# Feed forward of a hybrid decoder layer: the first product by seven products of quarters in six of eight chunks, and both products in two parts of sixteen column blocks

## The chip, the cores and the metric

The kernel runs on one core of a Trainium2 chip. The metric is the device time of one execution in microseconds (us). The engines are named as in the profile: PE is TensorE, PEld its weight load, DVE is VectorE, ACT is ScalarE, POOL is GpSimd, SP is SyncE, which only issues DMAs.

## What is computed

One decoder layer on 2048 prompt tokens and 64 sample tokens of width 1024, in fp32. A mixer (a gated linear recurrence beside a short convolution) is followed by a LayerNorm, and that by a dense feed forward with 4096 hidden columns:

```python
    mix = jnp.einsum('btm,md->btd', jnp.concatenate([o.astype(x.dtype), yc], axis=-1), w_out)
    x = _layer_norm(ALPHA * x + mix, ln1_g, ln1_b)

    hid = jnp.square(jax.nn.relu(jnp.einsum('btd,df->btf', x, w_ff1)))
    x = _layer_norm(ALPHA * x + jnp.einsum('btf,fd->btd', hid, w_ff2), ln2_g, ln2_b)
```

The states of the recurrence and of the convolution are outputs too.

## The kernel before

**Tiling.** The prompt goes in four blocks of 512 tokens (`b` from 0 to 3); the sample's 64 tokens ride with block 1. Each block runs a mixer stage (projections `m1` to `m3` with the recurrence between them, then the output projection in two passes of two token tiles) and a feed forward stage. Precision: each fp32 operand is split into a high part (fp32r) and the rest, and each product is three matmuls (`mm3`, L230 to L232: high by high, high by low, low by high; `mm3_on`, L236 to L238, in the second product).

**Weights.** All weights come as units of 128 x 1024, in the order in which `add_unit` lists them. For each unit SP loads 512 KB into `st` (three buffers), ACT copies the high part to `wh` (L194, four buffers), and DVE subtracts to get `wl` (L201, four buffers). `weights(u)` keeps this three units ahead of PE.

**First product, before.** A unit is a column block `f` of 128 hidden columns, 32 in all, in eight chunks of four. The first eight blocks go in two passes of 256 tokens (`f0`, since the LayerNorm of the later token tiles is still under way), the other 24 in one pass of 512 tokens (in block 1: 256 and then 320, with the sample), eight `k` steps of three matmuls each. ACT takes relu and square of the result out of PSUM into `raw` (L1008, L1010), which holds a chunk as four slots (two halves of tokens by two halves of hidden columns) of 2 x 256 columns.

**Second product.** It is done by seven products of quarters instead of eight (`PRODUCTS`): tokens, hidden columns and output columns are halved, sums of quarters of the hidden values are multiplied with sums of quarters of the weights, and the results are added into the outputs with signs (`INTO`). The order is step by step, B21, B11, T4, T2, T1, B22, T3, each over all eight chunks, so that a step's two PSUM banks collect over the chunks. For each (step, chunk), `prepare` runs two products ahead: ACT copies a slot's high part `h` (L1040), POOL subtracts to get `l` (L1041), and DVE forms the next sum of hidden values in place (L1045, L1047, L1049; L990 forms the first when a chunk is done). At the end of a step DVE adds its banks into the residual (L1069, L1072).

**Sums of weights.** The sums T1 to T4 of quarters of the second weights are made once, in block 0, in DRAM: POOL issues eight DMAs per chunk, copies (L331) and accumulating DMAs (L329), 64 in all, two of them after each step of the mixer's main loop from step 4 on (`next(making, 0)`). They share POOL's queue with its instructions, which run in order: the inverse root in the recurrence's output norm (L683), that of the LayerNorm (L262), and `l`. Eight DMAs are in flight at most, since they take turns on eight semaphores and each waits for the one before it on its own.

**LayerNorm.** `norm_steps` gives ACT the scaling (L857), PE the transposes (L864) and DVE gain and bias of the transposed values (L867, L868), placed by hand between PE's units (`lnq`). The residual gets gain and bias on DVE in the second `f0` pass (`affine`, L913).

Of the kernel before, what the change touches and what calls it, by code (L numbers as in the profile page):

```python
# [13 lines left out]
ALU = mybir.AluOpType  # L14
# [34 lines left out]
X_PLACES = (("B21", 2), ("B21", 5), ("B11", 2), ("B11", 5), ("B22", 5))  # L49
# [4 lines left out]
def hybrid_step(ctx, tc, a, o):  # L54
# [111 lines left out]
    def unit_dma():  # L166
        src, _, cols, _, _ = units[at["dma"]]
        st = TOK() if at["dma"] < 6 else new((P, D), "st", 3)
        if at["dma"] < 2:
            for half in (slice(0, D // 2), slice(D // 2, D)):  # L170
                nc.sync.dma_start(st[:, half], src[:, half])
        else:
            nc.sync.dma_start(st[:, :cols], src)
        stages[at["dma"]] = st
        at["dma"] += 1
# [143 lines left out]
    sums = [{k: scratch.tile([P, D], F32, tag=f"{k}_{c}", bufs=1, name=f"{k}_{c}") for k in SUMS} for c in range(NCH)]  # L319

    def make_sums():
        def at(c, k):
            return a["w_ff2"][c * 4 + RAW[k]] if k in RAW else sums[c][k]

        for to, of, acc in (("T1", "B11", False), ("T3", "B22", False), ("T1", "B12", True), ("T3", "B12", True),
                            ("T2", "T3", False), ("T2", "B11", True), ("T4", "T2", False), ("T4", "B21", True)):
            for c in range(NCH):
                if acc:
                    g.dma_start(at(c, to), at(c, of), accum_op=ALU.add, max_dma_last_dim=4096)  # L329
                else:  # L330
                    g.dma_start(at(c, to), at(c, of), max_dma_last_dim=4096)  # L331
                yield
# [3 lines left out]
    for b in range(NB):  # L336
# [14 lines left out]
        pl["ff1"] = [(f, add_unit(a["w_ff1"][f])) for f in range(nf, NF)]  # L351
        pl["ff2"] = []
        pl["nc"] = NCH - 1 if b == NB - 1 else NCH
        nx = x_units(b + 1) if b + 1 < NB else []
        for step, _ in PRODUCTS:
            for c in range(pl["nc"]):
                pl["ff2"].append((step, c, add_unit(a["w_ff2"][c * 4 + RAW[step]] if step in RAW else sums[c][step])))
                if (step, c) in X_PLACES and nx:
                    src, cols, use = nx.pop(0)
                    add_unit(src, cols=cols, use=use)  # L360
# [11 lines left out]
    for b in range(NB):  # L372
# [468 lines left out]
        x1 = {}  # L841
# [3 lines left out]
        def norm_steps(tl):  # L845
# [13 lines left out]
            def flip(t, i):  # L859
# [5 lines left out]
                tmp = tmps[t, i] = TMP()  # L865
# [39 lines left out]
        affined = set()  # L905

        def affine(t, dh):
            if (t, dh) in affined:
                return
            affined.add((t, dh))  # L910
            z = x1[t][:tsz[t], dh * 512:dh * 512 + 512]
            for i, op in enumerate((ALU.mult, ALU.add)):
                v.tensor_tensor(z, z, lnb[:tsz[t], i, dh * 512:dh * 512 + 512], op)  # L913
# [65 lines left out]
        ncs = pl["nc"]  # L979
# [5 lines left out]
        rs = [TOK().rearrange("p (f t) -> p f t", t=NS) for _ in range(2)] if samp else None  # L985
# [6 lines left out]
        def ff1(f, w, sg):  # L992
# [3 lines left out]
            if c not in raw:  # L996

                raw[c] = F((P, 4, 2, 256), "raw", NCH)
            r = raw[c][:, 2 * odd:2 * odd + 2, q, :]
# [5 lines left out]
            a0, a1 = sg[0][0], sg[-1][0] + sg[-1][1]  # L1005
            for (c0, n), ps in zip(sg, banks):
                h0, h1 = c0 // 256, min(c0 + n, TB) // 256
                s.activation(r[:, h0:h1], ps[:, :256 * (h1 - h0)].rearrange("p (s t) -> p s t", t=256), AF.Relu)  # L1008
            h0, h1 = a0 // 256, min(a1, TB) // 256
            s.activation(r[:, h0:h1], r[:, h0:h1], AF.Square)  # L1010
            if a1 > TB:
                z = rs[f // 16][:, f % 16, :]
                s.activation(z, banks[-1][:, TB - sg[-1][0]:a1 - sg[-1][0]], AF.Relu)
                s.activation(z, z, AF.Square)
            written[c] += a1 - a0
            if written[c] == 4 * ncols and c < ncs:
                chunk_done(c)
            after()

# [4 lines left out]
        flush()  # L1024
        for t, dh in ((2, 0), (3, 0), (0, 0), (1, 0), (2, 1), (3, 1), (0, 1), (1, 1), (4, 0), (4, 1)):
            if t < nt:
                lnq += [([lambda t=t, dh=dh: affine(t, dh)], [])]
        for f, w in twice(pl["f0"], 1):
            ff1(f, w, [(256, ncols - 256)])

        queue = [(step, c) for step, c, _ in pl["ff2"]]
# [20 lines left out]

        for i, (f, u) in enumerate(pl["ff1"]):
            if i >= len(pl["ff1"]) - 2:
                prepare()
            ff1(f, weights(u), segs)
        drain()
        norm_weights(1)
        if b == 0:
            for _ in making:  # L1060
                pass
# [24 lines left out]
        spairs = []  # L1086
        squeue = [c * FC + 2 * SAMPLE[step][0] for step, c, _ in pl["ff2"] if samp and step in SAMPLE]

        def sample_rows():
            if squeue:  # L1090
                f = squeue.pop(0)
                hp = F((P, 2, P), "hp", 2, F32R)
                split(hp[:, :, 0:NS], hp[:, :, NS:P], rs[f // 16][:, f % 16:f % 16 + 2, :])
                spairs.append(hp)

        to = dict(PRODUCTS)
        banks = {}
        sample_rows()
        for step, c, u in pl["ff2"]:
            w = weights(u)  # L1100
            parts = [tuple(x[:, q * 512:q * 512 + 512] for x in w) for q in range(2)]
            prepare()
            if step in SAMPLE:
                sample_rows()
            if step == "T3" and pl["last"] and 2 <= c < 6:
                if c == 2:
                    last = [F((P, 4, 2, 256), "raw", NCH, F32R) for _ in range(2)]
                split(last[0][:, c - 2], last[1][:, c - 2], raw[NCH - 1][:, c - 2])
            k = to[step]
            first = k not in banks  # L1110
            if first:
                banks[k] = [PS() for _ in range(2)]
            h, l = hid.pop((step, c))
            for p in range(2):
                cs = slice(p * P, p * P + P)
                for q, (rh, rl) in enumerate(parts):
                    mm3_on(banks[k][p], h[:, q, cs], l[:, q, cs], rh, rl, first and q == 0, c == ncs - 1 and q == 1)
            if samp and step in SAMPLE:
                if c == 0:
                    ys = PS()  # L1120
                hp = spairs.pop(0)
                for q, (rh, rl) in enumerate(parts):
                    mm_pair(ys, hp[:, q, :], rh, rl, c == 0 and q == 0, c == ncs - 1 and q == 1)
            if c == ncs - 1:
                for t0, dh, sign in INTO[k][step]:
                    for p in range(2):
                        add_to(t0 + p, dh, banks[k][p], sign)
                if samp and step in SAMPLE:
                    sample_sums(ys, SAMPLE[step][1])
# [138 lines left out]
```

## Time and profile before

| | |
|---|---|
| time, median of 3 runs | 2449.0 us (2446.64 to 2449.62) |
| the profiled execution's own time | 2449.19 us |
| its span, first to last instruction | 2447.4 us |
| PE busy | 2400.3 us (98%), 12876 matmuls |
| DVE, ACT, POOL busy | 1542.2, 1114.9, 524.9 us |
| first product of block 0 in one pass | 304 to 434 us |
| second product of block 0 | 434 to 593 us |

The profile is one execution. Matmuls are pipelined, and a matmul's shown length is longer than the distance to the next, so what a stage costs is read from the distance between starts of like instructions, not from busy time. A wait is put down to what ended last. The timeline gives start, length, engine, line and tiles of an instruction, merged where several of one kind follow each other (x8); the waiting time before it and what ended it stand in brackets.

### The profile page before, as it was taken

To read this page: it belongs to the slowest core of one execution; us is meant where nothing else is said; L and a number is where in the kernel's file an instruction comes from. 1 tells how busy PE (TensorE), PEld (TensorE's weight loads), DVE (VectorE), ACT (ScalarE), POOL (GpSimd) and SP (SyncE) were. 2 spreads that over 40 slices of the span, in tenths; PEclk is the share of its full clock that TensorE was granted. 3 is DMA by queue.
4 is the path that set the end of the run, shared out by engine and by line. 5 is a ranking of instruction groups with operands and counts; after the bars stand their busy time and mean duration, and the time that the engine had idled before them with its cause. 6 is when DMAs were issued, how large, how long until landed. Compare 5 with 4: busy or idle time off the path is not lost. (4 is left out here: it accounts for less than half of the span.)

```text
span 2447.4 us, 32997 instructions
## 1 busy us (share of the span) xinstructions
PE 2400.3 (98%) x12876; PEld 2051.5 (84%) x12876; DVE 1542.2 (63%) x2153; ACT 1114.9 (46%) x1794; POOL 524.9 (21%) x376
## 2 busy tenths in 40 slices
PE   7999999999999999999999999999999999999998
PEld 5888988878889889998778888988878888988876
DVE  5756822696865684227968857623886865822597
ACT  4334534654324354445554244534654334543553
POOL 3210000654001110004750000001662001000554
PEclk9999999999999999999999999999999999999999
DMA  9985423655223633225543225423654324433453
GB/s 329 277 233 174 160 97 112 199 186 179 79 78 75 211 121 104 87 96 164 180 149 118 91 80 190 144 96 129 206 188 146 104 82 159 161 103 116 163 184 113
DMA packets 103548, 358.79 MB, mean 147 GB/s; under 512 B 11552, under 2 KB 16032, under 8 KB 103392
## 3 DMA queue, kind: packets, MB, share of 16 engines
q1 hardware_dynamic: 91216, 313.88, 38.6%
q0 software_dynamic: 12032, 42.54, 6.5%
q8 instruction: 101, 1.65, 0.3%
q14 instruction: 55, 0.45, 0.1%
q10 hardware_dynamic: 144, 0.26, 0.0%
HBM read 345.59 MB, written 44.60 MB: 159 GB/s over the span
## 5 line engine op out<-in xcount | busy, mean ns | idle before, releaser
L201 DVE TENSOR_TENSOR wl<-st,wh 128x1024 fp32r<-128x1024 f32 x514 | 679.5, 1325 | 548.3 <-ACT wh L194 547.5
L230 PE MATMUL ps<-X,wh 128*128 128x512 f32 (+2 forms) x2272 | 779.6, 343 | 14.2 <-ACT X L155 11.0
L232 PE MATMUL ps<-X,wl 128*128 128x512 f32 (+2 forms) x2272 | 769.4, 339 | 1.0 <-DVE wl L201 1.0
L231 PE MATMUL ps<-X,wh 128*128 128x512 f32 (+2 forms) x2272 | 769.4, 339 | 0.5 <-DVE X L156 0.5
L194 ACT ACTIVATE wh<-st 128x1024 fp32r<-128x1024 f32 x515 | 543.1, 1055 | 381.0 <-DMA st<-T 90.8
L1041 POOL TENSOR_TENSOR l<-raw,h 128x512 fp32r<-128x512 f32 x217 | 391.6, 1808 | 947.3 <-ACT h L1040 930.9
L230 PEld LDWEIGHTS ps<-X,wh 128*128 128x128 f32 x2272 | 431.6, 190 | 60.6 <-ACT X L155 13.0
L232 PEld LDWEIGHTS ps<-X,wl 128*128 128x128 f32 x2272 | 431.3, 190 | 43.7 <-DVE wl L201 1.9
L231 PEld LDWEIGHTS ps<-X,wh 128*128 128x128 f32 x2272 | 431.7, 190 | 42.1 <-DVE X L156 2.6
L238 PE MATMUL ps<-wh,l 128*128 128x512 f32 x868 | 342.1, 394 | 8.9 <-POOL l L1041 8.9
L236 PE MATMUL ps<-wh,h 128*128 128x512 f32 x868 | 339.1, 391 | 6.3 <-DVE tok L1072 5.0
L237 PE MATMUL ps<-wl,h 128*128 128x512 f32 x868 | 339.2, 391 | 1.6 <-DVE wl L201 1.6
L1008 ACT ACTIVATE raw<-ps 128x256 f32<-128x256 f32 (+1 forms) x184 | 85.7, 466 | 372.6 <-PE ps L232 370.9
L238 PEld LDWEIGHTS ps<-wh,l 128*128 128x128 f32 x868 | 163.3, 188 | 53.1 <-POOL l L1041 19.9
L236 PEld LDWEIGHTS ps<-wh,h 128*128 128x128 f32 x868 | 163.4, 188 | 40.7 <-issue 6.2
L237 PEld LDWEIGHTS ps<-wl,h 128*128 128x128 f32 x868 | 163.2, 188 | 37.4 <-DVE wl L201 3.3
L1040 ACT ACTIVATE h<-raw 128x512 fp32r<-128x512 f32 x217 | 133.5, 615 | 7.7 <-PE ps L237 5.7
L262 POOL TENSOR_TENSOR sm<-sm,nhalf 128x1 f32<-128x1 f32 (+1 forms) x34 | 36.5, 1075 | 383.4 <-DVE sm L261 383.4
L230 PE MATMUL ps<-wh,X 128*128 128x512 f32 x256 | 104.0, 406 | 0.0
L230 PE MATMUL ps<-wh,S 128*128 128x512 f32 x256 | 101.3, 396 | 0.0
L232 PE MATMUL ps<-wh,X 128*128 128x512 f32 x256 | 100.3, 392 | 0.0
L232 PE MATMUL ps<-wh,S 128*128 128x512 f32 x256 | 99.9, 390 | 0.0
(204 smaller groups left out, 2560.4 us busy)
## 6 DMA issues: line engine op xcount, KB each, us to landing
st<-in_w_ff SPq DMA_DIRECT2D x249, 512.0 KB, 3.3
st<-T SPq DMA_DIRECT2D x124, 512.0 KB, 3.3
st<-in_w_in SPq DMA_DIRECT2D x110, 512.0 KB, 3.3
st<-in_w_out SPq DMA_DIRECT2D x56, 512.0 KB, 4.3
T<-in_w_ff POOLq DMA_DIRECT2D x48, 512.0 KB, 19.7
T<-T POOLq DMA_DIRECT2D x16, 512.0 KB, 17.8
lnb<-in_lnb SPq DMA_DIRECT2D x16, 512.0 KB, 5.9
tok<-in_x SPq DMA_DIRECT2D x16, 512.0 KB, 6.9
```

The source lines that it names most:

```text
L194: s.activation(wh, st, AF.Copy)
L201: v.tensor_tensor(wl, st, wh.bitcast(F32), ALU.subtract)
L230: te.matmul(out, lh, rh, start=first, stop=False)
L231: te.matmul(out, lh, rl, start=False, stop=False)
L232: te.matmul(out, ll, rh, start=False, stop=last)
L236: te.matmul(out, lh, rh, start=first, stop=False, skip_group_check=True)
L237: te.matmul(out, lh, rl, start=False, stop=False, skip_group_check=True)
L238: te.matmul(out, ll, rh, start=False, stop=last, skip_group_check=True)
L262: g.tensor_tensor(st[:n, 15:16], st[:n, 14:15], nhalf[:n, 0:1], ALU.pow)
L1008: s.activation(r[:, h0:h1], ps[:, :256 * (h1 - h0)].rearrange("p (s t) -> p s t", t=256), AF.Relu)
L1040: s.activation(h, x, AF.Copy)
L1041: g.tensor_tensor(l, x, h.bitcast(F32), ALU.subtract)
```

## The change

- **First product.** The eight column blocks of chunks 0 and 1 (`NPLAIN = 2`) stay as they were. Chunks 2 to 7 go by the same seven products of quarters: the 1024 inputs, the four column blocks of a chunk and the 512 tokens are halved. Each product is a unit (eight groups of three matmuls, 256 tokens wide, or 320 with the sample in four of the seven), so 24 units of a block become 42. Results are combined on their way out of PSUM (`ff1_product`): copies with sign on ACT, additions on DVE, relu and square in one DVE instruction or two on ACT.
- **Sums of tokens.** In the second `f0` pass `sum_steps` forms the sums of quarters of the LayerNorm's output on DVE and splits them.
- **Sums of weights.** The same eight steps of sums are made for six chunks of the first weights, from rows of half the length, ahead of those of the second weights: 112 DMAs instead of 64, chunks 2 and 3 first. They begin two main loop steps later (`i >= 6`).
- **Two parts.** The feed forward runs as two parts of four chunks (`NPART = 4`): first product of chunks 2 and 3, second product of chunks 0 to 3, first of 4 to 7, second of 4 to 7. Each step's banks are added to the residual once a part. `raw` has four buffers instead of eight.
- **Residual's gain and bias** (`affine`) move from DVE to POOL, beside the first eight products.

The line numbers shift: L201 is L206 after the change, L683 is L706, L262 is L267, L1041 is L1197, L913 is L937, L331 and L329 are L347 and L345.

**POOL, block 0, end of the mixer.** What stands on its queue around the output norm's inverse roots, before (`T_6`, `T_7` are sums of chunks 6 and 7, `sm` small tiles):

```order
L329 DMA T_5_104<-in_w_ff 128x1024
L329 DMA T_6_108<-in_w_ff 128x1024
L329 DMA T_7_112<-in_w_ff 128x1024
L683 ISA
L683 TENSOR_TENSOR sm_1459<-sm_1459,nhalf 128x4
L683 TENSOR_TENSOR sm_1490<-sm_1490,nhalf 128x4
L683 TENSOR_TENSOR sm_1530<-sm_1530,nhalf 128x4
L683 TENSOR_TENSOR sm_1570<-sm_1570,nhalf 128x4
L262 TENSOR_TENSOR sm_1937<-sm_1937,nhalf 128x1
```

and after (`T_b` are sums of the second weights, `T_a` of the first):

```order
L345 DMA T_b_116<-in_w_ff 128x1024
L345 DMA T_b_120<-in_w_ff 128x1024
L706 ISA
L706 TENSOR_TENSOR sm_1505<-sm_1505,nhalf 128x4
L345 DMA T_b_124<-in_w_ff 128x1024
L345 DMA T_b_128<-in_w_ff 128x1024
L706 TENSOR_TENSOR sm_1536<-sm_1536,nhalf 128x4
L347 DMA T_b_129<-in_w_ff 128x1024
L347 DMA T_b_133<-in_w_ff 128x1024
L706 TENSOR_TENSOR sm_1578<-sm_1578,nhalf 128x4
L347 DMA T_b_137<-in_w_ff 128x1024
```

The first of the four now stands behind 78 sums, with two more ahead of each of the others; sixteen more follow the last, so that the LayerNorm's first L267 stands behind 100.

**POOL, block 0, from the first product to the second.** Before, the LayerNorm's last inverse roots are followed at once by the `l` of the second product:

```order
L262 TENSOR_TENSOR sm_2143<-sm_2143,nhalf 128x1
L262 TENSOR_TENSOR sm_2185<-sm_2185,nhalf 128x1
L1041 TENSOR_TENSOR l_3467<-raw_2149,h_3466 128x512
L1041 TENSOR_TENSOR l_3504<-raw_2311,h_3503 128x512
L1041 TENSOR_TENSOR l_3553<-raw_2735,h_3552 128x512
```

and after, from the second `l` of part one on:

```order
L1197 TENSOR_TENSOR l_3244<-raw_2378,h_3243 128x512
L345 DMA T_b_130<-in_w_ff 128x1024
L345 DMA T_b_134<-in_w_ff 128x1024
L345 DMA T_b_138<-in_w_ff 128x1024
L345 DMA T_b_142<-in_w_ff 128x1024
L347 DMA T_b_132<-T_b_130 128x1024
L347 DMA T_b_136<-T_b_134 128x1024
L347 DMA T_b_140<-T_b_138 128x1024
L347 DMA T_b_144<-T_b_142 128x1024
L345 DMA T_b_132<-in_w_ff 128x1024
L345 DMA T_b_136<-in_w_ff 128x1024
L345 DMA T_b_140<-in_w_ff 128x1024
```

One more DMA follows and then the third `l`: the last twelve sums (for chunks 4 to 7) stand between the second and the third.

The diff, cut to its core:

```diff
-X_PLACES = (("B21", 2), ("B21", 5), ("B11", 2), ("B11", 5), ("B22", 5))
+X_PLACES = (("B21", 4), ("B21", 6), ("B11", 4), ("B11", 6), ("B22", 5))
+NPLAIN = 2
+NPART = 4
...
     def make_sums():
...
+        for at, cs in ((quarter1, range(NPLAIN, NPART)), (quarter1, range(NPART, NCH)),
+                       (quarter2, range(NPART)), (quarter2, range(NPART, NCH))):
+            for to, of, acc in (("T1", "B11", False), ("T3", "B22", False), ("T1", "B12", True), ("T3", "B12", True),
+                                ("T2", "T3", False), ("T2", "B11", True), ("T4", "T2", False), ("T4", "B21", True)):
+                for c in cs:
+                    if acc:
+                        g.dma_start(at(c, to), at(c, of), accum_op=ALU.add, max_dma_last_dim=4096)
+                    else:
+                        g.dma_start(at(c, to), at(c, of), max_dma_last_dim=4096)
+                    yield
...
-            if b == 0 and i >= 4:
+            if b == 0 and i >= 6:
                 next(making, 0)
                 next(making, 0)
...
             for i, op in enumerate((ALU.mult, ALU.add)):
-                v.tensor_tensor(z, z, lnb[:tsz[t], i, dh * 512:dh * 512 + 512], op)
+                g.tensor_tensor(z, z, lnb[:tsz[t], i, dh * 512:dh * 512 + 512], op)
...
+        def ff1_product(step, c, w):
...
+            for kk in range(4):
+                for q in range(2):
+                    cs = slice(q * 512 + kk * P, q * 512 + kk * P + P)
+                    mm3_on(banks_[q][:, :n], wh[:, cs], wl[:, cs], xh_[:, kk, :n], xl_[:, kk, :n],
+                           first and kk == 0 and (q == 0 or len(banks_) == 2), kk == 3)
...
+        for part, (ff1_units, ff2_units) in enumerate(pl["parts"]):
+            queue += [(step, c) for step, c, _ in ff2_units]
+            for i, (step, c, u) in enumerate(ff1_units):
+                if i >= len(ff1_units) - 2:
+                    prepare()
+                ff1_product(step, c, weights(u))
+            drain()
+            if part == 0:
+                norm_weights(1)
+                if b == 0:
+                    for _ in making:
+                        pass
...
+            for step, c, u in ff2_units:
```

More of the change, by code (lines that the diff above doesn't have):

```diff
@@ L978, in hybrid_step, with sample_values, values @@
         raw, hid, written = {}, {}, [0] * NCH
-        ncs = pl["nc"]
         def F(shape, tag, bufs, dt=F32):
             return new(shape, tag, bufs, dt, phase["of"])
-        rs = [TOK().rearrange("p (f t) -> p f t", t=NS) for _ in range(2)] if samp else None
+        rs = {}
+        def sample_values(c, f):
+            part = c // NPART
+            if part not in rs:
+                rs[part] = TOK().rearrange("p (f t) -> p f t", t=NS)
+            return rs[part][:, f % (NPART * FC):f % (NPART * FC) + 2, :]
+        def values(c):
+            if c not in raw:
+                raw[c] = F((P, 4, 2, 256), "raw", NPART)
+            return raw[c]
         def chunk_done(c):
@@ new lines, in sum_steps, with parts, wide @@
+        def sum_steps():
+            (h0, h1), (l0, l1) = ([x[:, :, 0:256] for x in y] for y in x1g)
+            sa = F((P, 2, 4, 256), "raw", NPART)
+            s1, s2 = sa[:, 0], sa[:, 1]
+            r1, r2 = xr[0][:, 0], xr[0][:, 1]
+            def parts(key, src, wide, half, tiles):
+                xq[key] = tiles
+                split(*(x[:, :, 0:256] for x in tiles), src)
+                if wide and samp:
+                    for x, y in zip(tiles, x1g):
+                        s.activation(x[:, :, 256:], y[half][:, :, TB:TB + NS].bitcast(F32), AF.Copy)
+            def wide():
+                return [F((P, 4, 256 + NS), "sw", 4, F32R) for _ in range(2)]
+            v.tensor_tensor(s1, h1, h0, ALU.subtract)
+            yield
+            v.tensor_tensor(s1, s1, l1, ALU.add)
+            v.tensor_tensor(s1, s1, l0, ALU.subtract)
+            yield
+            parts("T1", s1, True, 0, wide())
+            v.scalar_tensor_tensor(s2, s1, -1.0, r1, ALU.mult, ALU.subtract)
+            yield
+            parts("T2", s2, False, 0, [TOK(F32R).rearrange("p (k t) -> p k t", k=4) for _ in range(2)])
+            v.scalar_tensor_tensor(r2, r2, -1.0, s2, ALU.mult, ALU.subtract)
+            yield
+            parts("B22", r2, True, 1, wide())
+            v.tensor_tensor(r1, r1, h0, ALU.subtract)
+            yield
+            v.tensor_tensor(r1, r1, l0, ALU.subtract)
+            parts("T3", r1, False, 0, [F((P, 4, 256), "sn", 2, F32R) for _ in range(2)])
+            xr.clear()
+            yield
@@ L1024, in hybrid_step @@
         flush()
+        making_sums = sum_steps()
+        for _ in range(6):
+            lnq += [([lambda: next(making_sums, 0)], [])]
+        for f, w in twice(pl["f0"], 1):
+            ff1(f, w, [(256, ncols - 256)])
+        drain()
         for t, dh in ((2, 0), (3, 0), (0, 0), (1, 0), (2, 1), (3, 1), (0, 1), (1, 1), (4, 0), (4, 1)):
@@ L1027, in hybrid_step @@
                 lnq += [([lambda t=t, dh=dh: affine(t, dh)], [])]
-        for f, w in twice(pl["f0"], 1):
-            ff1(f, w, [(256, ncols - 256)])
-        queue = [(step, c) for step, c, _ in pl["ff2"]]
+        queue = []
         def prepare():
@@ L1099, in hybrid_step @@
[L1099 to L1127, printed above, removed]
-                if samp and step in SAMPLE:
-                    sample_sums(ys, SAMPLE[step][1])
```

219 lines of the change are left out of this document (158 added, 61 removed).

## The prediction

> **What bounds the kernel now.** I read the page, then the profile by windows, then the timeline of the engines that the change loads.
>
> ```profile
> span 2447.4 us, 32997 instructions
> PE 2400.3 (98%) x12876; PEld 2051.5 (84%) x12876; DVE 1542.2 (63%) x2153; ACT 1114.9 (46%) x1794; POOL 524.9 (21%) x376
> DMA  9985423655223633225543225423654324433453
> ```
>
> TensorE is busy 98% of the span, so time falls only if TensorE issues less, and any new wait of TensorE adds to it. But the DMA engines are full in the first two to three of forty slices, the first 150 us or so. This is where the weight sums are built. How far apart matmuls are is read from ScalarE, which takes a finished unit out of PSUM (timeline of ScalarE: start, length, instruction):
>
> ```profile
> 300.58 0.38 ACT L1008 ACTIVATE raw<-ps 128x256 f32<-128x256 f32 x1 [1.10 <-PE ps L232]
> 303.46 0.38 ACT L1008 ACTIVATE raw<-ps 128x256 f32<-128x256 f32 x1 [1.10 <-PE ps L232]
> 308.92 0.60 ACT L1008 ACTIVATE raw<-ps 128x512 f32<-128x512 f32 x1 [3.68 <-PE ps L232]
> 314.36 0.60 ACT L1008 ACTIVATE raw<-ps 128x512 f32<-128x512 f32 x1 [3.23 <-PE ps L232]
> ...
> 940.45 0.39 ACT L1008 ACTIVATE raw<-ps 128x256 f32<-128x256 f32 x1 [1.33 <-PE ps L232]
> 943.97 0.39 ACT L1008 ACTIVATE raw<-ps 128x256 f32<-128x256 f32 x1 [1.34 <-PE ps L232]
> 949.93 0.83 ACT L1008 ACTIVATE raw<-ps 128x256 f32<-128x256 f32 x2 [3.77 <-PE ps L232]
> 956.33 0.83 ACT L1008 ACTIVATE raw<-ps 128x256 f32<-128x256 f32 x2 [3.56 <-PE ps L232]
> ```
>
> Each step is 24 matmuls, or twice 24 in the last pair: 256 wide 2.88 us, 512 wide 5.44, 320 wide 3.52, 256 and 320 together 6.40. So 256 columns cost 0.120 us, and twice that is 6% over the 0.227 us of 512.
>
> **Removed: TensorE work.** In blocks 0, 2 and 3, 24 units of 5.44 us (130.6) become 6 x 7 products of 2.88 us (121.0), 9.6 us less in each. In block 1 (with the sample) 24 x 6.40 = 153.6 becomes 24 x 3.52 + 18 x 2.88 = 136.3, 17.3 us less. In all 3 x 9.6 + 17.3 = **46.1 us**. The second product keeps its matmuls.
>
> The Trainium skill ("TensorE: Matmul & The Clock Gate", section "Back-to-back issue gap") has a rule against this: weight load and matmul together set the spacing, about 81 ns at 128 columns and 131 at 512. An estimate on the straight line between gives 98 ns at 256, by which the change would lengthen each first product; the rows above (0.120 against 0.227) say otherwise, so this way gets no chance.
>
> **Added: 48 more sums on GpSimd's queue in block 0.** GpSimd's timeline and the DMA tables:
>
> ```profile
> 1.34 4.30 POOL L331 DMA_DIRECT2D T<-in_w_ff  x8 [0.32 <-issue]
> 7.85 0.52 POOL L331 DMA_DIRECT2D T<-in_w_ff  x1 [2.22 <-DMA T<-in_w_ff]
> ...
> 22.87 0.52 POOL L331 DMA_DIRECT2D T<-in_w_ff  x1 [0.91 <-DMA T<-in_w_ff]
> ...
> 43.54 0.81 POOL L329 DMA_DIRECT2D T<-in_w_ff  x1 [2.83 <-DMA T<-in_w_ff]
> ...
> 67.72 0.81 POOL L329 DMA_DIRECT2D T<-in_w_ff  x1 [2.01 <-DMA T<-in_w_ff]
> ...
> 145.59 0.81 POOL L329 DMA_DIRECT2D T<-in_w_ff  x1 [1.79 <-DMA T<-T]
> 174.36 1.88 POOL L683 TENSOR_TENSOR sm<-sm,nhalf 128x4 f32<-128x4 f32 x1 [27.95 <-DVE sm L682]
> ...
> 234.36 0.55 POOL L262 TENSOR_TENSOR sm<-sm,nhalf 128x1 f32<-128x1 f32 x1 [43.81 <-DVE sm L261]
> ```
>
> ```profile
> q0 software_dynamic: 12032, 42.54, 6.5%
> ...
> T<-in_w_ff POOLq DMA_DIRECT2D x48, 512.0 KB, 19.7
> ...
> out_y<-tok POOLq DMA_DIRECT2D x12, 512.0 KB, 3.0
> ...
> out_y<-tok SPq DMA_DIRECT2D x7, 256.0 KB, 2.0
> ```
>
> Eight are in flight, and each later issue waits for the landing of one before it. Issues that wait on copies come (22.87 - 7.85) / 7 = 2.15 us apart, those on accumulations (67.72 - 43.54) / 7 = 3.45. The last of 64 lands near 145.59 + 19.7, say 168 us. Their work: queue 0 took 6.5% of 2447.4 = 159 us of all sixteen engines for 42.54 MB; the 64 sums are 33.55 MB of it, 125 us, so **1.96 us each**.
>
> GpSimd now meets its first L683 (L706 in the new code) behind 78 sums and its first L262 (L267) behind 100; before, both stood behind 64 that had landed. The hundredth waits until 96 have landed: 32 x 1.96 = 63 us of DMA work more than the 64. The 36 sums that touch quarters of the first weights go in rows half as long. That costs nothing if bytes count and 36 x 1.96 = 70 us if rows do; The output's halves from SP, 256 KB in such rows, land in 2.0 us against 3.0 for 512 KB in as many whole rows, so bytes count for most, and I take 5. The weights' own loads need, by the DMA share (columns: length, busy time of PE, its weight load, DVE, ACT, POOL, each with its count, clock, DMA share, GB/s):
>
> ```profile
> 175.00:200.00 25.00, 25.00 (x143) 21.54 (x142) 12.65 (x23) 15.11 (x52) 5.18 (x4) 1.00 0.26 88
> 200.00:215.00 15.00, 15.00 (x68) 12.39 (x67) 7.82 (x10) 5.28 (x6) 0.00 (x0) 1.00 0.57 208
> 215.00:235.00 20.00, 20.00 (x90) 16.57 (x89) 11.09 (x15) 5.89 (x6) 0.55 (x1) 1.00 0.68 236
> ...
> 435.00:457.00 22.00, 22.00 (x99) 18.19 (x98) 16.00 (x12) 14.95 (x20) 14.64 (x8) 1.00 0.67 209
> ```
>
> 6.5 + 8.6 + 13.6 us, and 1.8 for 168 to 175: 30.5. So L262 runs at 168 + 63 + 5 + 30 = 266 instead of 234: 32 us late. What hangs on both:
>
> ```profile
> 188.96 0.81 PE L692 MATMUL ps<-ident,S 128*128 128x128 f32 x5
> ...
> 235.65 1.23 ACT L857 ACTIVATE tok<-tok,sm 128x1024 f32<-128x1024 f32 x1
> ...
> L864 PE MATMUL ps<-ident,tok x32: 270/272/273, 239.9 to 274.4; 128*128 128x128 f32 x32
> ```
>
> L262 releases ScalarE's L857, done at 236.9, and behind L857 wait ScalarE's next weight splits; TensorE's transposes L864, which stand in its order in the middle of the output projection, start at 239.9. The slack is 3 us, so TensorE loses **29 us**. Half of it falls earlier: L683 waits for 74 landed sums (10 x 1.96 + 4 for short rows, and 8 for loads: 168 + 32 = 200 against 174), and ScalarE's scaling behind it, its own weight splits and TensorE's L692 with it; L692 starts at 188.96, some 10 us after it could (L683 ends at 176.2, and an estimated 2 to 3 us of ScalarE and VectorE lie between). What is lost there is part of the 29. Ends: 15, if the loads yield to the sums by half, and 29 + 65 with rows counting. SP's loads of the new sums pass no queue that holds them: chunks 2 and 3 are summed first.
>
> **Moved: twelve sums ahead of the second product.** They stand on GpSimd's queue between the second and the third `l` of block 0. Four accumulations, four copies that wait for them, four accumulations that wait for the copies. From 2.15 and 3.45 scaled to a mean of 1.96: 1.5 and 2.4 us of transfer. The first lands after about 4.5 (3.0 alone, a slower transfer, the issue), the fourth at 11.7, the copies from 13.2 to 17.7, the last issue ends at 18.5 and the third `l` (1.29 below) at 20; loads at share 0.67 add up to 4. Two `l` are ready, so TensorE needs it two products (12 matmuls of 0.227 us each, 2.72) and two matmuls later, at 5.9. It loses 14 to 18, I take **16** (6 if transfers overlap wholly, 20 at the first stage's pace).
>
> **Second product in two parts.** VectorE, by windows and by line in 479 to 545:
>
> ```profile
> 479.00:501.00 22.00, 21.71 (x96) 17.98 (x97) 21.73 (x18) 13.10 (x18) 14.14 (x9) 1.00 0.55 177
> 501.00:523.00 22.00, 21.38 (x91) 16.38 (x90) 22.00 (x19) 11.34 (x15) 10.05 (x7) 1.00 0.56 188
> 523.00:545.00 22.00, 21.06 (x90) 16.14 (x89) 22.00 (x18) 12.71 (x17) 12.14 (x9) 1.00 0.57 186
> ```
>
> ```profile
> L201 DVE TENSOR_TENSOR wl<-st,wh 128x1024 fp32r<-128x1024 f32 x23 | 41.8, 1818 | 0.0
> L1045 DVE SCALAR_TENSOR_TENSOR raw<-raw 128x512 f32<-128x512 f32 x8 | 12.0, 1504 | 1.2 <-POOL l L1041 1.2
> L1072 DVE SCALAR_TENSOR_TENSOR tok<-tok,ps 128x512 f32<-128x512 f32 x4 | 2.5, 675 | 0.0
> ```
>
> VectorE is full through T4, T2 and T1 (21.73, 22.00, 22.00 of 22), and TensorE idles 0.3, 0.6 and 0.9 us. Each part closes its banks with sixteen additions of 0.68 us, so a block gets sixteen more, eight of them (5.4 us) in that full stretch. But each part enters it after a slack one (16.00 of 22 in B21) and three units ahead. I take 2 us a block, **8** in all; ends 0 and 22.
>
> **First product's new vector work.** LayerNorm's scaling (L913) goes from VectorE to GpSimd beside the first eight products, in all sixteen instructions a block.
>
> ```profile
> L194 ACT ACTIVATE wh<-st 128x1024 fp32r<-128x1024 f32 x515 | 543.1, 1055 | 381.0 <-DMA st<-T 90.8
> ...
> L913 DVE TENSOR_TENSOR tok<-tok,lnb 128x512 f32<-128x512 f32 x64 | 43.7, 689 | 1.1
> ```
>
> ```profile
> 425.03 1.29 POOL L1041 TENSOR_TENSOR l<-raw,h 128x512 fp32r<-128x512 f32 x1 [160.74 <-ACT h L1040]
> ...
> L201 DVE TENSOR_TENSOR wl<-st,wh 128x1024 fp32r<-128x1024 f32 x22 | 27.2, 1236 | 90.7 <-ACT wh L194 90.7
> ```
>
> A chunk's seven products are 20.2 us of TensorE. VectorE then has seven splits, two squares that read SBUF alone, four additions out of PSUM and one difference: with GpSimd idle 7 x 1.24 + 7 x 0.68 = 13.4; at the durations beside a working GpSimd 7 x 1.82 + 2 x 1.50 + 5 x 0.68 = 19.1. Still below 20.2, so hidden but for edges: 1 us a block, **4**; ends 0 and 35 (the second rival). ScalarE has 7 x 1.06 for splits, four copies of 0.60 and two passes of a whole slot pair (1.06 each): 11.9. Loads come every 2.88 us, no denser than the second product's 2.72. The token sums take eleven VectorE instructions of 1.24 us, 13.6, under the second pass of 256 columns, where sixteen L913 of 0.69, 11.0, leave.
>
> **Sum:** -46.1 + 29 + 16 + 8 + 4 = +10.9. The profiled execution took 2449.19, the median is 2449.0, so **2460 us**. A measurement of this kernel can tell some 0.2%, 5 us, from no change.
>
> **Rivals.** *The sums are done in time (faster).* If GpSimd reaches L683 and L262 as early as now, only 16 + 8 + 4 stand against 46.1: 2431 us. Place: GpSimd's queue in block 0. It decides at the pace: 96 landed by 234 instead of 266 needs 32 us less of 188, 1.6 us a sum. For it: the mean of 1.96 includes other transfers of that queue. Against: the observed paces of 2.15 and 3.45 leave no room. 0.20.
>
> *VectorE becomes the bound (much slower).* If splits and GpSimd's instructions exclude each other, chunk 2 has 14 x 1.29 = 18.1 us of GpSimd and 11 of VectorE's SBUF work in 20.2 us: 8.9 late a block, 35 in all, 2491 us. For it: L201 grows from 1.24 to 1.82. Against: the second product holds its pace with both. 0.09. The Trainium skill ("SBUF — State Buffer", section "Who interferes with whom") states such an exclusive lock for a VectorE instruction with two SBUF inputs; the growth of L201 agrees in kind.
>
> *Short rows cost whole packets:* +65, 2525 us, 0.05. *Losses at their low ends* (15, 6, few us) meet the gain: near 2430 to 2449, I put it at no change, 0.08. That the products are not shorter is excluded by the rows above.
>
> **How the numbers follow.** Forecast 0.58, of which 0.05 ends within 5 us of 2449. Faster 0.20; same 0.08 + 0.05 = 0.13; slower 0.53 + 0.09 + 0.05 = 0.67. The range 2428 to 2490 holds the forecast's own ends, the no-change case, most of the faster one and half of the VectorE one; about 0.15 is left out.
>
> **What would show it.** Right: in block 0 the first L706 near 200 and L267 near 266, TensorE idle before L692 and L864; a gap of some 16 us after the second product of the second matmul stage; products 2.88 us apart; DMA full to about 260. Wrong: L267 near 235, or no gap at the third `l`, or products over 2.9 us apart with VectorE at 22 of 22.

## The result, and the profile after

The changed kernel takes 2554.1 us, median of 4 runs (2552.29 to 2559.95), beside 2447.8 for the kernel before, measured along with it: a ratio of 1.0441, 95% interval 1.0418 to 1.0464. The forecast was 2460, 2428 to 2490: the sign is right, the size is not. To the 106 us that it lost come the 46 us that TensorE's shorter products should have given, so about 152 us have to be found. (In ratios, which are used below because the kernel before differs by some 5 us between chips: 0.0441 x 2448 = 108.)

The page of the changed kernel, and from TensorE's waits (us in total, times, longest):

```profile
span 2558.2 us, 36164 instructions
PE 2389.6 (93%) x14028; PEld 2086.0 (82%) x14028; DVE 1816.3 (71%) x2479; ACT 1186.5 (46%) x1812; POOL 681.7 (27%) x492
PE   7995896998999997999989999999999999999997
PEclk9997998999999998999999999999999999999999
DMA  9999748555422452544454224465555324355553
q0 software_dynamic: 22016, 67.71, 10.6%
```

```profile
PE ps L243 <- POOL l L1197: 41.6, 26, 20.1
PE ps L715 <- DVE S L711: 26.8, 2, 24.2
PE ps L235 <- ACT X L160: 24.7, 8, 11.4
PE ps L241 <- ACT raw L1124: 13.4, 18, 1.3
PE ps L236 <- DVE X L161: 10.5, 5, 2.8
```

TensorE falls from 98% to 93%. The lowest slices after the first (5, 6 and 7 tenths) are the fourth and the seventh, in block 0, and the sixteenth, where block 1's feed forward begins, and in the same three the granted clock is below 9 tenths. About 10 us of the waits for X L160 come at the very start, where the kernel before has them too. The waits for L1124, here ScalarE's copy of T1's bank, are new and were not in the forecast.

The products themselves came as forecast. ScalarE takes them out 2.88 us apart, here T2 and T1 of one chunk (block 2; start, length, instruction):

```profile
1804.57 0.60 ACT L1124 ACTIVATE raw<-ps 128x512 f32<-128x512 f32 x1 [1.34 <-PE ps L243]
...
1807.44 0.60 ACT L1124 ACTIVATE raw<-ps 128x512 f32<-128x512 f32 x1 [1.25 <-PE ps L243]
```

A chunk of seven products takes longer than seven times 2.88, 20.16 us: B22's first matmuls of three chunks start at 1808.09, 1829.19 and 1850.29, 21.10 us apart, since each waits for that copy (e2).

**Block 0's mixer.** GpSimd's timeline: the first L706 (forecast near 200), the last sums of the mixer and L267 (forecast near 266). Behind it TensorE's wait, and two windows of the time after it (length, busy time of PE, its weight load, DVE, ACT, POOL, each with its count, clock, DMA share, GB/s).

```profile
209.67 1.37 POOL L706 TENSOR_TENSOR sm<-sm,nhalf 128x4 f32<-128x4 f32 x1
...
260.43 0.54 POOL L347 DMA_DIRECT2D T_b<-T_b  x1 [18.50 <-DMA T_b<-in_w_ff]
...
272.81 0.52 POOL L347 DMA_DIRECT2D T_b<-T_b  x1 [4.26 <-DMA T_b<-in_w_ff]
279.01 0.57 POOL L267 TENSOR_TENSOR sm<-sm,nhalf 128x1 f32<-128x1 f32 x1 [5.69 <-DVE sm L266]
```

```profile
212.99 1.12 PE L715 MATMUL ps<-ident,S 128*128 128x128 f32 x4 [24.23 <-DVE S L711]
```

```profile
230.00:255.00 25.00, 21.42 (x88) 17.09 (x87) 8.30 (x10) 4.51 (x5) 4.03 (x5) 0.93 1.04 310
255.00:280.00 25.00, 20.25 (x86) 15.45 (x84) 10.70 (x16) 5.58 (x5) 2.67 (x5) 1.00 1.04 335
```

The first L706 follows the 78th sum at once, 35 us later than the 174.36 of before. TensorE's L715 hangs on it through ScalarE and VectorE and starts 24 us late (188.96 before); with a second wait of 2.6 us the output projection starts 29 us late (238.75 against 210.00). So the forecast's 29 us are lost here already, where it had put half of them.

L267 runs 45 us later than the 234.36 of before, not 32, but not because of the sums ahead of it on GpSimd's queue: the last of them is issued at 272.81, and GpSimd then waits 5.69 us for VectorE's L266. The other 16 us are lost in the output projection. The DMA engines are full there (share 1.04, and 0.68 before), and between 238 and 280 us ScalarE waits 25.5 us for the projection's weights, which share these engines with the sums.

Queue 0 shows the size of the sums: 10.6% of 2558.2 is 271 us of all sixteen engines, against 159 before; 112 us for 48 sums are 2.34 us each, if all of it is put down to them, where the forecast had 1.96. That is 48 x 0.38 = 18 us more than at the forecast's price. All 48 stand ahead of the first L706, where the forecast had 4 us for short rows; it came 10 us later than 200.

**The seam.** GpSimd between the second and the third `l` of block 0, and TensorE behind it:

```profile
393.82 1.29 POOL L1197 TENSOR_TENSOR l<-raw,h 128x512 fp32r<-128x512 f32 x1 [0.17 <-ACT h L1196]
395.06 3.40 POOL L345 DMA_DIRECT2D T_b<-in_w_ff  x4
402.81 0.55 POOL L347 DMA_DIRECT2D T_b<-T_b  x1 [4.36 <-DMA T_b<-in_w_ff]
...
422.27 3.99 POOL L1197 TENSOR_TENSOR l<-raw,h 128x512 fp32r<-128x512 f32 x3
```

```profile
423.87 0.79 PE L243 MATMUL ps<-wh,l 128*128 128x512 f32 x1 [20.12 <-POOL l L1197]
424.46 0.63 PE L241 MATMUL ps<-wh,h 128*128 128x512 f32 x1
424.89 0.63 PE L242 MATMUL ps<-wl,h 128*128 128x512 f32 x1
...
428.26 0.39 PE L241 MATMUL ps<-wh,h 128*128 128x512 f32 x1
428.49 0.39 PE L242 MATMUL ps<-wl,h 128*128 128x512 f32 x1
```

The wait is 20.1 us, the upper end that the forecast gave. Behind it the matmuls start 0.43 us apart, and 0.23 only from 428.26 on: here the stall cost TensorE its own length and some 2 us at half clock.

**The two passes of 256 columns, block 1.** A window of the changed kernel from the end of the first pass into the second (columns as above), then VectorE's and GpSimd's groups in it (busy us, mean ns), and TensorE at the start of the second pass:

```profile
983.00:1013.00 30.00, 16.87 (x111) 16.12 (x110) 29.76 (x24) 10.77 (x21) 29.37 (x17) 0.72 0.22 72
```

```profile
L206 DVE TENSOR_TENSOR wl<-st,wh 128x1024 fp32r<-128x1024 f32 x4 | 8.1, 2022 | 0.0
L161 DVE TENSOR_TENSOR X<-raw,X 128x512 fp32r<-128x512 f32 x4 | 5.9, 1484 | 0.0
...
L896 DVE TENSOR_TENSOR raw<-ps,small 128x512 f32<-128x512 f32 x3 | 2.0, 677 | 0.0
```

```profile
L937 POOL TENSOR_TENSOR tok<-tok,lnb 128x512 f32<-128x512 f32 x15 | 26.4, 1777 | 0.6
```

```profile
1003.87 0.64 PE L235 MATMUL ps<-X,wh 128*128 128x320 f32 x1 [11.40 <-ACT X L160]
1006.24 0.63 PE L236 MATMUL ps<-X,wh 128*128 128x320 f32 x1 [1.73 <-DVE X L161]
```

GpSimd's gain and offset (L937) run from 980.45 to 1017.7, ahead of the first products and not beside them: nothing on GpSimd's queue keeps them back, and they start while TensorE is still in the first pass, which ends near 992.5. VectorE has next to no idle time (29.76 of 30 us busy), and the second half of the block's tokens (`X` of L160 and L161) comes late.

### The profile page after: what moved, and what is told of

Its sections match the earlier page's. It is cut to its first block, busy times and chain, and to the rows that moved or that the text cites. A ratio compares the mean times of both kernels' runs of the same rounds, so it can differ in the third digit from the quotient of the medians.

```text
span 2558.2 us, 36164 instructions
## 1 busy us (share of the span) xinstructions
PE 2389.6 (93%) x14028; PEld 2086.0 (82%) x14028; DVE 1816.3 (71%) x2479; ACT 1186.5 (46%) x1812; POOL 681.7 (27%) x492
## 3 DMA queue, kind: packets, MB, share of 16 engines
q0 software_dynamic: 22016, 67.71, 10.6%
## 5 line engine op out<-in xcount | busy, mean ns | idle before, releaser
L206 DVE TENSOR_TENSOR wl<-st,wh 128x1024 fp32r<-128x1024 f32 x586 | 771.1, 1324 | 177.9 <-ACT wh L199 176.3
L199 ACT ACTIVATE wh<-st 128x1024 fp32r<-128x1024 f32 x587 | 619.8, 1056 | 504.4 <-PE ps L243 118.9
L1197 POOL TENSOR_TENSOR l<-raw,h 128x512 fp32r<-128x512 f32 x217 | 377.4, 1747 | 855.7 <-ACT h L1196 844.4
L235 PE MATMUL ps<-X,wh 128*128 128x256 f32 (+2 forms) x1312 | 445.0, 339 | 26.6 <-ACT X L160 24.7
L236 PE MATMUL ps<-X,wh 128*128 128x256 f32 (+2 forms) x1312 | 434.9, 331 | 10.5 <-DVE X L161 10.5
L237 PE MATMUL ps<-X,wl 128*128 128x256 f32 (+2 forms) x1312 | 434.9, 331 | 2.0 <-DVE wl L206 2.0
L235 PEld LDWEIGHTS ps<-X,wh 128*128 128x128 f32 x1312 | 253.4, 193 | 51.0 <-ACT X L160 27.4
L236 PEld LDWEIGHTS ps<-X,wh 128*128 128x128 f32 x1312 | 253.5, 193 | 30.6 <-DVE X L161 13.3
L237 PEld LDWEIGHTS ps<-X,wl 128*128 128x128 f32 x1312 | 253.0, 193 | 23.2 <-DVE wl L206 3.9
L243 PE MATMUL ps<-X,wl 128*128 128x256 f32 (+1 forms) x576 | 166.0, 288 | 0.8 <-DVE wl L206 0.8
L242 PE MATMUL ps<-X,wh 128*128 128x256 f32 (+1 forms) x576 | 165.5, 287 | 0.0
L241 PE MATMUL ps<-X,wh 128*128 128x256 f32 (+1 forms) x576 | 165.5, 287 | 0.0
L1126 DVE TENSOR_TENSOR raw<-raw,ps 128x512 f32<-128x512 f32 (+1 forms) x120 | 66.4, 579 | 106.8 <-PE ps L243 106.0
L937 POOL TENSOR_TENSOR tok<-tok,lnb 128x512 f32<-128x512 f32 (+1 forms) x68 | 131.8, 1953 | 13.1 <-issue 8.8
L267 POOL TENSOR_TENSOR sm<-sm,nhalf 128x1 f32<-128x1 f32 (+1 forms) x34 | 37.6, 1106 | 344.9 <-DVE sm L266 344.9
```

Source lines behind the costliest of these rows:

```text
L199: s.activation(wh, st, AF.Copy)
L206: v.tensor_tensor(wl, st, wh.bitcast(F32), ALU.subtract)
L235: te.matmul(out, lh, rh, start=first, stop=False)
L236: te.matmul(out, lh, rl, start=False, stop=False)
L237: te.matmul(out, ll, rh, start=False, stop=last)
L241: te.matmul(out, lh, rh, start=first, stop=False, skip_group_check=True)
```

## Experiments

Prices are differences of ratios to the kernel before; each ratio has an interval of some 0.002 to either side, so a price below about 7 us is not sure.

### First weights' sums left out (e1)

```
 def quarter1(c, k):
+    k = {"T1": "B11", "T2": "B21", "T3": "B12", "T4": "B22"}.get(k, k)
...
-    for at, cs in ((quarter1, range(NPLAIN, NPART)), (quarter1, range(NPART, NCH)),
-                   (quarter2, range(NPART)), (quarter2, range(NPART, NCH))):
+    for at, cs in ((quarter2, range(NPART)), (quarter2, range(NPART, NCH))):
```

> The sums of the first weights are left out: the products T1 to T4 of the first product load raw quarters of the same size instead, so that the output is not the reference's, and GpSimd's DMA queue builds the 64 sums of the second weights alone, as before the change. Theory (the 48 added sums cost what block 0's mixer and the seam between its two products lost in the trace, 45 + 20 us, and TensorE's clock recovers with them): block 0's mixer ends again near 258.5 us, no wait of 20 us at the third l, 2554 - 68 = 2486 us. The forecast's sizes (29 + 16): 2509. Rival (VectorE and GpSimd are the bound all through, the sums only move the waiting): over 2540.

2492.0 us, 1.0174 (1.0159 to 1.0189): 65 us less. GpSimd's timeline of this run:

```profile
178.11 1.88 POOL L706 TENSOR_TENSOR sm<-sm,nhalf 128x4 f32<-128x4 f32 x1 [19.18 <-DVE sm L705]
...
238.11 0.55 POOL L267 TENSOR_TENSOR sm<-sm,nhalf 128x1 f32<-128x1 f32 x1 [43.81 <-DVE sm L266]
```

L267 is 41 us earlier, the waits for S L711 and for tok L880 are gone, and the longest for `l` is 2.0 us. The 4 us that stay to the 234.36 of before lie at the very start: at 34 us TensorE waits 4.5 us for a unit of weights, where the changed kernel waits 0.4 (at 31.9). The theory holds, and the rival is out.

### T1 ahead of T2 in the first product (e2)

```
+PRODUCTS1 = tuple(PRODUCTS[i] for i in (0, 1, 2, 4, 3, 5, 6))
...
-    ff1 += [(step, c, add_unit(quarter1(c, step))) for step, _ in PRODUCTS]
+    ff1 += [(step, c, add_unit(quarter1(c, step))) for step, _ in PRODUCTS1]
```

> In the first product alone T1 comes before T2, so that T2, in another bank, lies between T1 and B22, which share one. Theory (TensorE waits for ScalarE's copy of T1's bank before each B22, 0.85 to 1.4 us a chunk, 5 us in each of blocks 0, 2 and 3, and rarely in block 1): 2554 - 15 = 2539 us, and no wait of B22's matmuls on that copy. Rival (whatever waits there would wait a product later all the same, since VectorE and ScalarE are behind anyway): 2552 to 2556.

2538.6 us, 1.0375 (1.0358 to 1.0393): 16 us, and the wait for T1's copy is gone from TensorE's list. In the changed kernel that copy starts at 1807.44 (above), and B22's first matmul waits for it:

```profile
1808.09 0.38 PE L241 MATMUL ps<-sw,wh 128*128 128x256 f32 x1 [0.69 <-ACT raw L1124]
```

### Gain and offset left out, held back, on VectorE (e3, e5, e12)

```
e3:  -lnq += [([lambda t=t, dh=dh: affine(t, dh)], [])]
e5:  +lnq += [([lambda: g.tensor_tensor(SM((P, 1)), values(1)[:, 1, 1, 255:256], nhalf[:, 0:1], ALU.mult)], [])]
      (ahead of the first affine)
e12: -g.tensor_tensor(z, z, lnb[:tsz[t], i, dh * 512:dh * 512 + 512], op)
     +v.tensor_tensor(z, z, lnb[:tsz[t], i, dh * 512:dh * 512 + 512], op)
```

> LayerNorm 1's gain and offset on the residual, now on GpSimd, are left out, so that the output is not the reference's. Theory (GpSimd starts them as soon as the first pass of 256 columns runs, beside VectorE's fullest stretch, and slows its splits and token sums, so that TensorE waits for the token halves at the start of the second pass): those waits go, some 14 us in block 1 and 4 to 7 in the others, with half clock behind each: 2554 - 28 = 2526 us; L206 and the token sums fall from 2.3 to 1.24 us. Rival (VectorE's token sums alone fill the second pass, whether GpSimd runs or not): 2546 or more.

> GpSimd gets one small instruction more ahead of LayerNorm's gain and offset, which reads what ScalarE writes last in the second pass of 256 columns. So its sixteen instructions (eighteen and two in block 1) can no longer run early, and run beside the first ten products, where the forecast had put them at 1 us a block. Theory (their place costs, not their work): nearly all of what leaving them out gave, 2554 - 25 = 2529 us, no wait for token halves at the start of the second pass. Rival (wherever GpSimd works, VectorE slows and TensorE waits; it only moves into the products): 2545 or more, with L206 near 1.8 us in the first products and waits of TensorE on it.

> Only LayerNorm's gain and offset go back to VectorE, in the same place of its order as GpSimd had them, ahead of the first products. Theory (VectorE has room for half of them there, as the forecast's 15 of 23 us say): 2554 - 30 for GpSimd's early start and + 12 for VectorE, 2536 us. Rival (VectorE is not the limit in the products): 2526, as if they were left out; or it is full: 2550.

2523.6 (1.0303), 2531.9 (1.0339, 1.0323 to 1.0354) and 2522.3 us (1.0321, 1.0306 to 1.0337): 34, 25 and 29 us. So it is mostly the place and not the work. The same work later on the same engine gives back 25 of 34. Beside the other 9 us stand longer waits of TensorE for T1's copy (19.4 us in all against 12.4 in e3), and in block 1 L206 takes 1776 ns beside L937. On VectorE, in the same place of the order, 29 come back; that is nearer to the rival (2526) than to my theory. VectorE's groups of e12 in the like 30 us of block 1 (977 to 1007, all being earlier by some 6 us):

```profile
L206 DVE TENSOR_TENSOR wl<-st,wh 128x1024 fp32r<-128x1024 f32 x7 | 8.6, 1223 | 4.9 <-ACT wh L199 4.8
...
L161 DVE TENSOR_TENSOR X<-raw,X 128x512 fp32r<-128x512 f32 x3 | 2.1, 684 | 0.0
L896 DVE TENSOR_TENSOR raw<-ps,small 128x512 f32<-128x512 f32 x3 | 2.0, 680 | 0.0
```

Beside GpSimd, L206 took 2022 ns and here 1223, L161 1484 and here 684. L896, whose one large input is in PSUM, took 677 and 680. What the Trainium skill ("SBUF — State Buffer", section "Who interferes with whom") says agrees with these rows: VectorE instructions with two inputs in SBUF contend with a GpSimd instruction that reads SBUF, and those with one do not.

### Token sums left out (e11)

```
-making_sums = sum_steps()
-for _ in range(6):
-    lnq += [([lambda: next(making_sums, 0)], [])]
+xq.update(T1=xq["B11"], T2=xq["T4"], B22=xq["B21"], T3=xq["T4"])
+xr.clear()
```

> The sums of token halves are left out: T1, T2, B22 and T3 of the first product take raw token halves, so that the output is not the reference's; LayerNorm's gain and offset stay on GpSimd, unheld. Theory (it takes both, the token sums on VectorE and GpSimd beside it, to make TensorE wait in the second pass of 256 columns): nearly what leaving out the gain and offset gave, 2554 - 25 = 2529 us. Rival (GpSimd's instructions alone slow VectorE enough): 2545 or more; or the token sums' vector work is dear by itself: under 2515.

2550.1 us, 1.0424 (1.0396 to 1.0451): 4 us, not told from none. The theory falls, and the rival holds: GpSimd's instructions alone slow VectorE enough, and the wait of 11.4 us for the second half of the tokens is still there. The token sums, 13.6 us of VectorE a block, are hidden as the forecast had it.

### Two parts alone (e4)

```
-    if c >= NPLAIN:
-        ff1 += [(step, c, add_unit(quarter1(c, step))) for step, _ in PRODUCTS]
+    if c >= NPLAIN:
+        ff1 += [(None, f, add_unit(a["w_ff1"][f])) for f in range(c * FC, c * FC + FC)]
...
-    ff1_product(step, c, weights(u))
+    ff1(c, weights(u), segs)
```

> The second product in two parts as in the changed kernel, but the first product plain in all chunks, without sums of first weights or of token halves, and LayerNorm's gain and offset on VectorE as before the change. Theory (two parts cost 8 us by the forecast, and some 15 us more because the loads of the next block's tokens crowd into the second part): 2470 us. Forecast's size alone: 2456. Rival (two parts are most of the loss, through the closing additions on a full VectorE): 2500 or more.

2473.3 us, 1.0102 (1.0083 to 1.0121): 25 us, three times the forecast's term. Of these 4.6 are there before the first part begins (L267 at 238.98 against 234.36), the same wait for weights at the start as in e1. The time is near the theory's, but its reason, the crowded loads, is not shown by it. What the list of waits shows is the closings, which now come twice a block: six waits and 11.4 us, three and 5.0 before. One of them comes where B22 goes on in the bank that T1 has just closed (the last matmul stage of block 2):

```profile
1865.33 0.47 PE L241 MATMUL ps<-wh,h 128*128 128x512 f32 x1 [2.38 <-DVE tok L1215]
...
1866.34 0.63 PE L242 MATMUL ps<-wl,h 128*128 128x512 f32 x1
1866.77 0.63 PE L243 MATMUL ps<-wh,l 128*128 128x512 f32 x1
```

### The twelve sums moved off the seam (e6)

```
 def ff1_product(step, c, w):
+    if b == 0:
+        next(making, 0)
```

> The twelve sums that stand between the second and the third l of block 0 are issued one ahead of each product of the first feed-forward stage's first part, in the same order. Theory (TensorE waits 20.1 us there for GpSimd's third l, and runs some 2 us at half clock behind it): 2554 - 22 = 2532 us. Forecast's size: 2538. Rival (the transfers collide with the products' loads there, the DMA engines being loaded to 0.6 already, and cost the same again): 2550.

2540.8 us, 1.0378 (1.0363 to 1.0394): 15 us. The wait of 20 us is gone (2.0 us is the longest for `l`). The price lies nearer to the forecast's 16 than to my 22.

### The tokens' loads spread (e7)

```
-X_PLACES = (("B21", 4), ("B21", 6), ("B11", 4), ("B11", 6), ("B22", 5))
+X_PLACES = (("B21", 5), ("B11", 5), ("T4", 5), ("B22", 4), ("B22", 7))
```

> The loads of the next block's tokens stand four products apart or more in the second part (B21 5, B11 5, T4 5, B22 4 and 7 instead of B21 4 and 6, B11 4 and 6, B22 5). Theory (two apart, three units of 512 KB are wanted in two products of 2.72 us, 289 GB/s where the trace never shows more than 228 there, and TensorE waits 0.5 to 1.1 us a product, some 7 us a block): half to two thirds of 3 x 7 us goes, 2542 us. Rival (the waits come from ScalarE's and VectorE's order in B21 and B11, not from the loads): 2551 to 2557; or the token splits now fall where VectorE is full, and the time grows: 2560.

2548.6 us, 1.0418 (1.04 to 1.0435): 6 us, between the two and below what can be told. Whether the loads' places matter stays open.

### The sums spread over block 0's feed forward (e8)

```
+    if c >= NPLAIN and b == 0:
+        ff1 += [(None, f, add_unit(a["w_ff1"][f])) for f in range(c * FC, c * FC + FC)]
...
+making1 = make_sums(((quarter1, range(NPLAIN, NCH)),))
...
+if b == 0 and j % 3 == 2:      (second product; also ahead of each unit of the second pass and each plain one)
+    next(making1, 0)
```

> The first product is plain in block 0 (512 columns, no sums of token halves there), so that the 48 sums of the first weights are first wanted in block 1; GpSimd's queue builds the second weights' 64 in the mixer as before the change, and issues the 48 one by one through block 0's feed forward, one ahead of each plain unit and of every third product. Theory (the sums cost only because they stand ahead of waiting work, not by their transfers): the time without them, 2492, and 9.6 us for block 0's wider product, less the token sums' VectorE work: 2500 us. Rival (the 96 us of transfers that they need take the loads' time wherever they are put): 2530 or more.

2527.8 us, 1.0320 (1.0302 to 1.0337): 30 us where 54 were expected. Block 0's mixer is short again, and a new wait stands at the start of its second product. GpSimd, SP's queue and ScalarE there:

```profile
350.91 3.64 POOL L939 TENSOR_TENSOR tok<-tok,lnb 128x512 f32<-128x512 f32 x2
354.49 1.06 POOL L344 DMA_DIRECT2D T_a<-in_w_ff  x1
...
356.35 4.02 POOL L939 TENSOR_TENSOR tok<-tok,lnb 128x512 f32<-128x512 f32 x2
```

```profile
340.41 0.33 SPq L178 DMA_DIRECT2D st<-in_w_ff  x1
358.15 2.58 SPq L259 DMA_DIRECT2D lnb<-in_lnb  x2
360.83 14.70 SPq L178 DMA_DIRECT2D st<-in_w_ff  x5
```

```profile
370.65 1.06 ACT L199 ACTIVATE wh<-st 128x1024 fp32r<-128x1024 f32 x1 [10.71 <-DMA st<-in_w_ff]
```

The gain and offset alternate with sums on GpSimd and so end at 360; SP's load of the next gains (L259), which overwrites theirs, waits for them; and five weights' loads wait behind it on SP's queue. TensorE waits 8.2 us for what hangs on this. So of the 24 us that are missing, these are not the transfers as such (the rival), but a third queue that GpSimd's order reaches; where the others went was not traced.

### All together (e9, e10)

Block 0 plain as in e8, with one sum ahead of each unit of the second pass and two ahead of each plain unit, none among the `l`; the sums of the second weights from the fourth step on; T1 ahead of T2; the loads as in e7. Gain and offset: in e9 on VectorE in block 0 and held on GpSimd in the others, in e10 on VectorE in all.

```
-if b == 0 and i >= 6:
+if b == 0 and i >= 4:
...
+if b == 0 and sg[0][0] + sg[0][1] > 256:
+    for _ in range(sg[0][1] // 256):
+        next(making1, 0)
```

> All that helped together: block 0 plain, the 48 sums of the first weights issued only beside its plain units (two ahead of each, one ahead of each unit of the second pass), where GpSimd has nothing else to do, and none among the l; the 64 sums started as before the change; T1 ahead of T2 in the first product; LayerNorm's gain and offset on VectorE in block 0 and held back on GpSimd in the others; the tokens' loads spread. Theory (the prices add): 2554 - 62 + 10 - 10 (T1 ahead of T2, two blocks instead of three) - 17 (held back, three blocks) - 6 - 4 (start of the sums) = 2465 us. Rival (the sums' transfers cost again, as they did one by one among the l): 2490. That it beats the kernel before (under 2443) would need the two parts' 25 us to shrink as well.

> As the kernel before it in this call, but LayerNorm's gain and offset on VectorE in all blocks, beside the first products. Theory (VectorE has some 15 of 23 us there, and 11 more are 26, so TensorE waits 3 us in each of three blocks, while GpSimd's slowing goes): 2470 us, within 8 of the other. Rival (two engines beat one: held back on GpSimd is better by 20): 2485.

2454.8 us, 1.0045 (1.0029 to 1.0061), and 2451.8, 1.0025 (1.0014 to 1.0036). Nearly the whole loss is gone, and more than the prices had added up to (2465). So the sums, placed so, seem to cost next to nothing; no run has all this without them. But 36.5 us of TensorE work less (46.1 without block 0) still give no gain.

### Block 0 whole, and the closing moved (e13, e14)

```
e13: -for part in range(NCH // NPART):
     +for cs in ((range(NCH),) if b == 0 else (range(NPART), range(NPART, NCH))):
e14: +pairs = [(step, c) for step, _ in PRODUCTS for c in cs]
     +pairs.remove(("T2", cs[-1]))
     +pairs.insert(pairs.index(("T1", cs[-1])) + 1, ("T2", cs[-1]))
```

> As the kernel with everything mended and LayerNorm's gain and offset on VectorE, but block 0 wholly as before the change: one part of eight chunks, the tokens' loads in their old places there. Theory (two parts cost block 0 some 12 us, in waits at the edges of the parts): 2452 - 12 = 2440 us, 0.9975 of the kernel before. Rival (what is left of the loss lies in the first product of blocks 1 to 3): 2450, no change.

> As the kernel before it in this call, and in the second product the last T2 comes after the last T1, so that a product on another bank lies between the closing of T1's bank, which VectorE empties, and B22, which goes on in it. Theory (TensorE waits there 2.2 us and runs 1.6 us more at half clock, twice a block): 7 closings of 2 to 4 us, 2440 - 15 = 2425 us, 0.992 of the kernel before. Rival (VectorE is behind there in any case, and the wait comes a product later): 2438.

2444.3 us, 0.9981 (0.9972 to 0.9990), as the theory had it, and 2435.5, 0.9953 (0.9938 to 0.9967): 7 us more, half of what was expected. The page of e14, and from its waits:

```profile
span 2432.1 us, 35128 instructions
PE 2369.3 (97%) x13596; PEld 2060.7 (85%) x13596; DVE 1745.5 (72%) x2466; ACT 1168.2 (48%) x1802; POOL 555.2 (23%) x424
```

```profile
PE ps L246 <- POOL l L1215: 15.1, 17, 2.3
PE ps L238 <- ACT X L163: 12.1, 3, 9.9
```

No wait for a closing is left. This version is faster than both kernels; against the one before it gains 0.5%.

## Why the forecast was wrong, step by step

- **TensorE's work, -46.1.** The size of a product is confirmed (2.88 us). That the work gives its gain once the waits are gone is shown for blocks 1 to 3 only in part: e14 has 36.5 us less and ends 12 us below the kernel before.
- **"TensorE loses 29 us" in block 0's mixer: the right queue, but too small, and partly on the wrong path.** L267 is 41 us later with the sums than without them (e1). "I take 5" for short rows failed: the 48 sums took 18 us more of the engines than at 1.96. And the step from "L262 runs at 266" to the loss failed: the 29 us go at L706, not half there and half at L267, and L267 does not wait for the hundredth sum. Another 16 us go because the output projection's weights come late through full DMA engines; the forecast counted these loads only as a delay of the sums. With all 48 sums away 65 us go, where both terms together had 45.
- **The twelve sums at the seam, 16.** Right in kind and near in size: 15 by e6. The wait itself was 20.1 us, at the end of the forecast's range.
- **Second product in two parts, 8.** Too small: 25 (e4), or 20 without the 4.6 at the start. The forecast counted VectorE's additions, and not that B22's first matmul waits for the closing of T1's bank, now twice a block; moving that gave 7 (e14), and block 0 wholly as before 11 (e10 to e13).
- **"beside the first eight products", 4.** This is the step that failed outright. An instruction moved to an idle engine starts when its inputs are there, not where its neighbours in the old order stand. GpSimd began the gain and offset in the first pass (980.45 in block 1), when VectorE had the second half of the tokens to prepare and next to no idle time. Price 25 to 34 (e3, e5, e12), against 1 us a block. The forecast's second rival had the mechanism, GpSimd and VectorE in each other's way, but looked for it among the `l` of the products; what it costs there was not measured alone, and between the two passes it decides.
- **The first product's edges.** "No denser than the second product" looked at loads and busy time, not at the banks: T1 and B22 share one, and 16 us go in waiting for ScalarE to empty it (e2). The forecast had no term for it.

By the prices, each taken alone, 65 + 16 + 29 + 25 = 135 of 154 us are found (108 and the 46 of the gain). The forecast had 45 for the sums, nothing for the first product's edges, 4 for gain and offset and 8 for the two parts. The other 19 have no edit of their own: TensorE's list in e9 shows waits of 1 to 3 us for `l`, hp and h. Whether these are VectorE's load alone was not tried. The signs that the forecast gave for being right came (a late L706 and L267, waits at the transposes, the gap at the third `l`, products 2.88 us apart), and the time was still far off: they covered only the losses that it had listed.

## What to carry to other kernels

An engine that is freed of waiting runs ahead: when work moves to an idle queue, ask when its inputs are ready, and whom it meets there, not beside whom it was written. Work that only later stages need (the 48 sums) cost next to nothing on a queue with nothing behind it, and was dear ahead of one small instruction that others wait for. A stage can also be late through the DMA engines that it shares with such work, and not only through the queue. And where a product goes on in the bank that the one before has just closed, put another bank's product between.

## What the runs showed of the hardware

- TensorE's clock fell to half in a stall and stayed there for a few us behind it. In the changed kernel the granted clock is 0.50 for 27 us around block 0's long wait, from 192.5 on, when the last matmul had started at 188.37. In the seam it is 0.51 from 407.5 on (403.36), and behind it ten matmuls stood 0.43 us apart instead of 0.23. Windows:

```profile
192.50:219.80 27.30, 4.23 (x14) 3.35 (x15) 4.78 (x8) 8.72 (x36) 15.63 (x22) 0.50 1.03 247
407.50:428.00 20.50, 4.13 (x10) 3.26 (x11) 2.45 (x2) 2.40 (x4) 8.04 (x9) 0.51 1.04 296
```

  The Trainium skill ("TensorE: Matmul & The Clock Gate", section on the HAM clock gate) says that the clock is halved after an idle window of some 3.4 us and full again after a busy one. The trace agrees for these two long waits. But shorter ones were enough too: behind the 2.38 us of e4 the matmuls from 1866.34 to 1869.33 stand 0.43 us apart, for some 3.4 us. No run kept TensorE busy through a stall, so the price by itself was not measured.
- VectorE's splits take 1.65 times as long beside GpSimd's reads (2022 against 1223 ns), the splits of 512 columns 2.2 times (1484 against 684), and the multiplication that reads PSUM (L896) no longer than alone (677 against 680).
- For the 48 sums of the first weights, three in four of them with rows of 2 KB, queue 0 took 112 us more of all sixteen engines, 2.34 us a sum, where its mean by bytes had been 1.96. How much of that is the rows was not measured alone.
